# Two squared-ReLU layers: the residual turned to tokens on partitions by VectorE block transposes and transfers

## The chip, the cores and the metric

The kernel runs on one core of one Trainium2 chip. The metric is the device time of one launch in microseconds (us). Before the change it is 1060.97 us, the median of three runs between 1060.56 and 1061.39.

A core has several engines, each with its own stream of instructions: TensorE (PE in the profile, its weight loads PEld), VectorE (DVE), ScalarE (ACT), GpSimd (POOL) and SyncE (SP), which in this kernel issues most of the transfers. SBUF is the memory on the core, with 128 partitions; PSUM holds the results of TensorE.

## The reference

Two layers on 512 tokens of width 1024. Each has a token mixer and then a squared-ReLU MLP, each behind an RMS norm and added to the residual; one norm stands at the end.

```python
for layer in range(DEPTH):                       # DEPTH = 2
    hn = rmsnorm(h, norm_mix[layer])
    if layer % 2 == 0:
        mix = chunked_band_attention(hn, ...)
    else:
        mix = rglru_block(hn, ...)
    h = h + mix
    h = h + sq_relu_mlp(rmsnorm(h, norm_mlp[layer]), mlp_w1[layer], mlp_w2[layer])
return rmsnorm(h, norm_final)

def rmsnorm(x, g):
    return x * rsqrt(mean(x * x, axis=-1) + 1e-6) * g

def sq_relu_mlp(h, w1, w2):                      # w1 1024 x 4096, w2 4096 x 1024
    z = relu(h @ w1)
    return (z * z) @ w2
```

Everything is float32.

## The kernel before

**Layout.** The residual h is kept with features on partitions: eight tiles `hT[k]` of 128 features x 512 tokens, four in each of the buffers `hx0` and `hx1` (in the profile `h`). For a product the value is split in two parts of a shorter float type, `hnH` by ScalarE (L237) and `hnL` by VectorE (L238), and so are all weights: a tile loaded by SP (`wr` or `b`, L120 and L128) is cast to `wh` on ScalarE (L140) and the rest `wl` is formed on VectorE (L143). A product then is three matmuls, high by high, high by low and low by high (`mm3`, L217 to L219). Weights are fetched five tiles ahead from one list, `plan`, in the order of use; the raw tiles of w2 lie in buffers b11, b21, b12 and b22 of the pool `sr`.

**The MLP of a layer** is `mlp(ly, norm)` (L603). `up(p, j)` (L636) is one product of 24 matmuls: 128 of the hidden columns for all 512 tokens, into a bank of PSUM called `u`; ScalarE takes ReLU and square (L643, L644). The norm's factor isn't applied to h: since relu(s h)^2 = s^2 relu(h)^2 for s > 0, the factor `rq` (s squared, one number per token) is applied when results are read. Eight `up`s make one round of four, `round_(p)`. A round multiplies by w2 in seven block products of a Strassen scheme, called "11", "12", "s1", "s4", "s2", "s3" and "22", of 24 matmuls each, on PSUM banks X, Y and Z with tokens on partitions. After each product `read` (L625) adds bank times `rq` into the tiles `d` (128 tokens x 512 features, `dt[t, c]`): four token blocks t, two halves c. In the three first rounds the `up`s of the next round stand between the steps.

**Residual and norm in layer 0 (before).** The first read of each `d` is a ScalarE copy with scale (L629), later reads are VectorE instructions (L631). The sum of squares of the norm is taken from `hT`: eight squares on ScalarE (L244, L247), seven adds on VectorE into `nm1acc` (L248), and small matmuls against a tile of ones (`tokens`, L261, `nm1ss`) which stand after `up(0, 3)`. At the end `turns` (L755) turns `d` back to features on partitions by 32 TensorE transposes (L767, banks `back0` and `back1`), and VectorE adds them to `hT` (L769). The next norm, `n1`, is made of the new `hT` in the same way: eight squares, seven adds, matmuls `n1ss` within the recurrent layer's first products `xb` (L261), and after them `rstd`.

**Residual and norm in layer 1 (before).** The output is wanted with tokens on partitions, so here the residual is turned at the layer's start: after each `up(0, j)`, `turn(t, c)` (L617) makes four TensorE transposes into a bank `hx` (L620), a ScalarE copy into `d` (L621) and a ScalarE square with a sum along the row into a column of `fs` (L623). After `up(0, 7)`, `rq` is formed of the columns. All reads are VectorE's.

**What sets the order.** The program is written in the order above. The Tile framework's scheduler places each instruction in its engine's stream and sets the semaphores; each engine runs its stream in order. A transfer that waits holds back all that stand behind it on SP.

Of the kernel before, what the change touches and what calls it, by code (L numbers as in the profile page):

```python
# [10 lines left out]
F32 = mybir.dt.float32  # L11
F32R = mybir.dt.float32r
AF = mybir.ActivationFunctionType
ALU = mybir.AluOpType
# [26 lines left out]
def trunk(ctx: ExitStack, tc: tile.TileContext, xT, cols, gfin, win, wqkv, wo, rwin, rga, rgx, rwo, w1, w2, out):  # L41
# [13 lines left out]
    def atp(name):  # L55
        return ps.tile([P, T], F32, name=name, tag="at")
# [44 lines left out]
    def fetch():  # L101
# [129 lines left out]
    class Norm:  # L231
# [41 lines left out]
        def inverse(self, total):  # L273
            V.tensor_scalar(rq, total, 1.0 / D, EPS, ALU.mult, ALU.add)
            V.reciprocal(rq, rq)

        def rstd(self):
            row = atp(f"{self.name}row")
            for t in range(4):
                PE.matmul(row[:, t * P : (t + 1) * P], rt[:, t : t + 1].to_broadcast([P, P]), ident, start=True, stop=True)  # L280
            r = self.both[:, 1]
            S.copy(r, row)
            return r
# [319 lines left out]
    def mlp(ly, norm):  # L603
        with ExitStack() as mctx:
# [11 lines left out]

            def turn(t, c):  # L617
                x = atp(f"hx{t}{c}")
                for m in range(4):
                    PE.transpose(x[:, m * P : (m + 1) * P], hT[4 * c + m][:, t * P : (t + 1) * P], ident)  # L620
                S.copy(dt[t, c], x)  # L621
                sq = wk.tile([P, T], F32, name=f"hsq{t}{c}", tag="nsq", bufs=2)
                S.activation(sq, x, AF.Square, accum_out=fs[:, 2 * t + c : 2 * t + c + 1])  # L623

            def read(acc, t, c):  # L625
                d, r = dt[t, c], rq[:, t : t + 1]
                if (t, c) in new:
                    new.remove((t, c))
                    S.activation(d, acc, AF.Copy, scale=r)  # L629
                else:  # L630
                    V.scalar_tensor_tensor(d, acc, r, d, ALU.mult, ALU.add)  # L631

# [3 lines left out]
            def up(p, j):  # L636
                if j % 4 == 0:
                    a[p, j // 4] = zp.tile([P, 2, 4, U], F32, name=f"a{ly}{p}{j}", tag=f"a{j // 4}")
                WH, WL = want(1)
                acc = mmp(f"u{ly}{p}{j}")  # L640
                project([acc], [slice(0, P)], WH, WL, xs)
                c = a[p, j // 4][:, :, j % 4, :]
                S.activation(c, acc.rearrange("p (h c) -> p h c", h=2), AF.Relu)  # L643
# [12 lines left out]
            def round_(p):  # L656
# [95 lines left out]
                step("22", X, False, 2, 0)  # L752


            def turns(step, product, X):  # L755
# [3 lines left out]
                def back(qs, h):  # L759
                    for q in qs:  # L760
# [25 lines left out]
                next(opening)  # L786
                for m in range(4, KT):
                    n1.square(m)
                for _ in open_x(1):
                    pass  # L790
                for m in range(4):
                    n1.square(m)


            def ends(step, product, X):
                gain = [gfins[:, c] for c in range(2)]
                total = lambda t: fs[:, 2 * t : 2 * t + 1]
                part = lambda t, c: fs[:, 2 * t + c : 2 * t + c + 1]

                def squares(t, c):  # L800
                    sq = wk.tile([P, T], F32, name=f"fsq{t}{c}", tag="nsq", bufs=2)
                    S.activation(sq, dt[t, c], AF.Square, accum_out=part(t, c))

# [70 lines left out]
    with ExitStack() as rctx:  # L874
# [83 lines left out]
        for u in range(4):  # L958
            WH, WL = want(2 if u > 1 else 1)
            for i in range(2):  # L960
# [5 lines left out]
                if c == 1:  # L966
                    n1.sums()
                if c == 2:
# [93 lines left out]
```

## Time and profile before

| | |
|---|---|
| median of three runs | 1060.97 us (1060.56 to 1061.39) |
| profiled execution | 1061.19 us |
| its span, first to last instruction | 1059.4 us |
| mean granted TensorE clock | 0.999 |
| TensorE matmuls | 1051.4 us busy, 4824 |
| VectorE | 795.4 us busy, 1174 |
| ScalarE | 587.1 us busy, 899 |
| transfers | 111.51 MB, 105 GB/s on the mean |

The times below are microseconds from the start of the span of that one execution. A row such as `L217 PE MATMUL u<-hnH,wh` names the line of the kernel, the engine, the operation and the tiles that it writes and reads. A row of the timeline begins with its start and its duration. Matmuls run into each other: the duration of one is longer than the distance of two starts.

The MLP of layer 0 runs on TensorE from 245.37, that of layer 1 from 721.93.

### The profile page before, as it was taken

To read this page: it belongs to the slowest core of one execution; us is meant where nothing else is said; L and a number is where in the kernel's file an instruction comes from. 1 tells how busy PE (TensorE), PEld (TensorE's weight loads), DVE (VectorE), ACT (ScalarE), POOL (GpSimd) and SP (SyncE) were. 2 spreads that over 40 slices of the span, in tenths; PEclk is the share of its full clock that TensorE was granted. 3 is DMA by queue.
4 is the path that set the end of the run, shared out by engine and by line. 5 is a ranking of instruction groups with operands and counts; after the bars stand their busy time and mean duration, and the time that the engine had idled before them with its cause. 6 is when DMAs were issued, how large, how long until landed. Compare 5 with 4: busy or idle time off the path is not lost.

```text
span 1059.4 us, 12872 instructions
## 1 busy us (share of the span) xinstructions
PE 1051.4 (99%) x4824; PEld 871.6 (82%) x4824; DVE 795.4 (75%) x1174; ACT 587.1 (55%) x899; POOL 10.1 (1%) x28
## 2 busy tenths in 40 slices
PE   9999999999999999999999999999999999999997
PEld 8888888888888888888888878888888888888886
DVE  6898779867395697587599799974397487577596
ACT  6677557646463564454456587545564454454454
POOL 1010000000000000000000000000000000000000
PEclk9999999999999999999999999999999999999999
DMA  8444353254046036026103222283136026125002
GB/s 263 118 129 130 80 176 103 76 163 160 21 127 188 5 98 200 21 80 199 40 1 115 85 80 86 67 288 97 40 92 200 27 80 198 41 79 179 1 1 80
DMA packets 128413, 111.51 MB, mean 105 GB/s; under 512 B 4320, under 2 KB 104672, under 8 KB 128352
## 3 DMA queue, kind: packets, MB, share of 16 engines
q1 hardware_dynamic: 127776, 109.99, 34.0%
q8 instruction: 38, 0.62, 0.2%
q10 hardware_dynamic: 576, 0.72, 0.2%
q14 instruction: 23, 0.19, 0.1%
HBM read 104.39 MB, written 2.10 MB: 101 GB/s over the span
## 4 chain that ended last, share of the span: by engine, by line
PE 97%; DVE 1%; ACT 1%; issue 0%; DMA 0%; POOL 0%; ACTq 0%; POOLq 0%
PE u L217 11%; PE u L219 11%; PE u L218 11%; PE x L217 6%; PE x L219 5%; PE x L218 5%; PE y L217 3%; PE y L218 3%; PE y L219 3%; PE x L439 2%; PE wo L217 1%; PE wo L218 1%; PE ro L219 1%; PE v L217 1%; PE ro L217 1%; PE xb L217 1%
## 5 line engine op out<-in xcount | busy, mean ns | idle before, releaser
L143 DVE TENSOR_TENSOR wl<-wr,wh 128x1024 fp32r<-128x1024 f32 (+1 forms) x122 | 146.5, 1202 | 98.0 <-ACT wh L140 89.6
L140 ACT CAST wh<-b 128x1024 fp32r<-128x1024 f32 x112 | 117.8, 1052 | 174.2 <-PE u L218 128.1
L140 ACT CAST wh<-wr 128x1024 fp32r<-128x1024 f32 (+1 forms) x121 | 125.6, 1040 | 145.4 <-PE u L218 63.4
L143 DVE TENSOR_TENSOR wl<-b,wh 128x1024 fp32r<-128x1024 f32 x112 | 136.6, 1220 | 91.1 <-ACT wh L140 91.0
L217 PE MATMUL u<-hnH,wh 128*128 128x512 f32 x512 | 200.1, 391 | 0.0
L219 PE MATMUL u<-hnH,wl 128*128 128x512 f32 x512 | 199.4, 389 | 0.0
L218 PE MATMUL u<-hnL,wh 128*128 128x512 f32 x512 | 199.2, 389 | 0.0
L219 PEld LDWEIGHTS u<-hnH,wl 128*128 128x128 f32 x512 | 96.1, 188 | 20.2
L218 PEld LDWEIGHTS u<-hnL,wh 128*128 128x128 f32 x512 | 96.2, 188 | 19.8
L217 PEld LDWEIGHTS u<-hnH,wh 128*128 128x128 f32 x512 | 96.1, 188 | 19.7
L138 DVE TENSOR_TENSOR b<-b,b 128x1024 f32<-128x1024 f32 x64 | 76.3, 1216 | 1.1 <-DMA b<-in_w 0.8
L217 PE MATMUL x<-wh,h 128*128 128x512 f32 (+1 forms) x132 | 50.8, 385 | 0.6 <-DVE d L836 0.6
L218 PE MATMUL x<-wl,h 128*128 128x512 f32 (+1 forms) x132 | 50.6, 384 | 0.0
L643 ACT ACTIVATE a<-u 128x512 f32<-128x512 f32 x64 | 37.8, 591 | 13.3 <-PE u L219 13.3
L631 DVE SCALAR_TENSOR_TENSOR d<-x,rq,d 128x512 f32<-128x512 f32 x59 | 42.0, 744 | 0.5 <-PE x L219 0.5
L644 ACT ACTIVATE a<-a 128x512 f32<-128x512 f32 x64 | 40.6, 635 | 1.7
L419 ACT ACTIVATE p<-p,mx 128x128 f32<-128x128 f32 (+1 forms) x64 | 35.2, 552 | 6.2 <-DVE mx L416 6.1
L667 ACT CAST h<-a 128x1024 fp32r<-128x1024 f32 (+2 forms) x34 | 27.2, 800 | 6.7 <-PE y L218 5.8
L412 DVE CUSTOM_DVE_ANT_0 p<-s,bias 128x128 f32<-128x128 f32 (+1 forms) x64 | 27.6, 484 | 3.2 <-PE s L409 2.9
L217 PEld LDWEIGHTS x<-wh,h 128*128 128x128 f32 x132 | 24.8, 188 | 5.5 <-DVE d L836 0.8
L443 ACT CAST pH<-x 128x512 fp32r<-128x512 f32 (+1 forms) x48 | 21.7, 517 | 13.5 <-PE x L439 13.3
L218 PEld LDWEIGHTS x<-wl,h 128*128 128x128 f32 x132 | 24.8, 188 | 4.8
(351 smaller groups left out, 2292.4 us busy)
## 6 DMA issues: line engine op xcount, KB each, us to landing
wr<-in_w SPq DMA_DIRECT2D x64, 512.0 KB, 4.1
b<-in_w SPq DMA_DIRECT2D x64, 512.0 KB, 4.3
wr<-in_wqkv SPq DMA_DIRECT2D x20, 512.0 KB, 4.0
wr<-in_rwin SPq DMA_DIRECT2D x16, 512.0 KB, 3.4
wr<-in_wo SPq DMA_DIRECT2D x8, 512.0 KB, 4.1
wr<-in_rwo SPq DMA_DIRECT2D x8, 512.0 KB, 3.5
x<-in_xT SPq DMA_DIRECT2D x8, 256.0 KB, 3.8
bias<-in_win SPq DMA_DIRECT2D x4, 512.0 KB, 4.7
```

The costliest lines, as they stand in the source:

```text
L138: V.tensor_sub(raw, raws[x, half], raws[y, half])
L140: S.copy(H[:, :n], raw[:, :n])
L143: low = V.tensor_sub(L[:, :n], raw[:, :n], f(H[:, :n]))
L217: PE.matmul(acc, WH, XH, start=start, stop=False, skip_group_check=more)
L218: PE.matmul(acc, WH, XL, start=False, stop=False, skip_group_check=more)
L219: PE.matmul(acc, WL, XH, start=False, stop=stop, skip_group_check=more)
L412: V.tensor_tensor_reduce(out=pt[:, seg[t] : seg[t] + n], in0=sc[t], in1=b[:, h % 4, T - n :], scale=1.0, scalar=-3.0e38, op0=ALU.add, op1= ...
L419: S.activation(pt[:, seg[t] : seg[t] + n], pt[:, seg[t] : seg[t] + n], AF.Exp, bias=mx[:, t : t + 1], accum_out=sm[:, t : t + 1],)
L631: V.scalar_tensor_tensor(d, acc, r, d, ALU.mult, ALU.add)
L643: S.activation(c, acc.rearrange("p (h c) -> p h c", h=2), AF.Relu)
L644: S.activation(c, c, AF.Square)
L667: S.copy(H[:, ks], raw[n][:, ks])
```

## The change

In both MLP layers the residual now is in `d` from the start.

- **Turning.** `turn()` stands after `up(0, 0)`. VectorE transposes `hT` in blocks of 32 x 32: 16 instructions of 128 partitions x 8 x 32 elements, into two tiles `turned`, which take the place of the raw weights b12 and b22 before these are loaded. A block transpose moves elements within 32 partitions only; 32 transfers on SP, SBUF to SBUF, 32 partitions x 2 x 256 elements each (64 KB), bring the blocks to the partitions of their tokens, into `res`, of which the tiles `dt[t, c]` are views. Within a token's row the features come out in another order; the host puts the rows and columns of the weights, the gains and the output in the order that fits (`once` for layer 1's input, `twice` for the end).
- **Norm sums.** Eight ScalarE squares of `d` with sums along the row into columns of `fs`, written in the program after `up(0, 5)`, and `rq` of them after `up(0, 6)`: in both layers. The norm `n1` takes its sums in the same way from the finished `d` at the end of layer 0, with one VectorE add of columns. So `nm1ss`, `n1ss`, `hx`, and the adds `nm1acc` and `n1acc` are gone.
- **Reads.** All reads are VectorE's, eight more in layer 0 and as many fewer on ScalarE.
- **Turning back.** The 32 TensorE transposes at the end of layer 0 stay. VectorE copies the result to `hT` instead of adding it.
- **Raw weights.** b11, b21, b12 and b22 are tiles of two halves each, instead of two tiles each.

```diff
+                    both = state["raw"].tile([P, 2, 1024], F32, name=f"b{name}_{i}", tag=f"b{name}")
                     for h in range(2):
-                        raws[name, h] = state["raw"].tile([P, 1024], F32, name=f"b{name}{h}_{i}", tag=f"b{name}{h}")
+                        raws[name, h] = both[:, h]
...
-        def sums(self):
-            S.activation(rt, self.tokens(), AF.Sqrt, bias=epsb, scale=1.0 / D)
+        def sums(self, total=None):
+            S.activation(rt, self.tokens() if total is None else total, AF.Sqrt, bias=epsb, scale=1.0 / D)
             V.reciprocal(rt, rt)
...
-            dt = {(t, c): dp.tile([P, T], F32, name=f"d{ly}{t}{c}", tag=f"d{t}{c}") for t in range(4) for c in range(2)}
-            new = set() if ly else set(dt)
+            res = dp.tile([P, 4, 2, T], F32, name=f"d{ly}", tag="d")
+            dt = {(t, c): res[:, t, c] for t in range(4) for c in range(2)}
...
-            def turn(t, c):
-                x = atp(f"hx{t}{c}")
-                for m in range(4):
-                    PE.transpose(x[:, m * P : (m + 1) * P], hT[4 * c + m][:, t * P : (t + 1) * P], ident)
-                S.copy(dt[t, c], x)
-                sq = wk.tile([P, T], F32, name=f"hsq{t}{c}", tag="nsq", bufs=2)
-                S.activation(sq, x, AF.Square, accum_out=fs[:, 2 * t + c : 2 * t + c + 1])
+            def turn():
+                blocks = [sr.tile([P, 2, 4, KT, 32], F32, name=f"turned{ly}{h}", tag=f"b{n}2") for h, n in enumerate((1, 2))]
+                for k in range(KT):
+                    for h in range(2):
+                        V.transpose(
+                            blocks[h].rearrange("p t j k a -> p (t j) k a")[:, :, k],
+                            hT[k][:, h * U : (h + 1) * U].rearrange("p (n b) -> p n b", b=32),
+                        )
+                for h in range(2):
+                    for i in range(4):
+                        for j in range(4):
+                            nc.sync.dma_start(
+                                res[32 * j : 32 * j + 32, 2 * h : 2 * h + 2, i // 2, (i % 2) * U : (i % 2 + 1) * U],
+                                blocks[h][32 * i : 32 * i + 32, :, j].rearrange("p t k a -> p t (k a)"),
+                            )
 
             def read(acc, t, c):
                 d, r = dt[t, c], rq[:, t : t + 1]
-                if (t, c) in new:
-                    new.remove((t, c))
-                    S.activation(d, acc, AF.Copy, scale=r)
-                else:
-                    V.scalar_tensor_tensor(d, acc, r, d, ALU.mult, ALU.add)
+                V.scalar_tensor_tensor(d, acc, r, d, ALU.mult, ALU.add)
...
-                if p == 0 and ly:
-                    turn(*divmod(j, 2))
-                if (ly, p, j) == (0, 0, 0):
-                    for k in range(KT):
-                        norm.square(k)
-                elif (ly, p, j) == (0, 0, 3):
-                    norm.inverse(norm.tokens())
-                elif (ly, p, j) == (1, 0, 7):
+                if (p, j) == (0, 0):
+                    turn()
+                if (p, j) == (0, 5):
+                    for t in range(4):
+                        for c in range(2):
+                            squares(t, c)
+                if (p, j) == (0, 6):
                     V.tensor_add(rq, fs[:, 0:8:2], fs[:, 1:8:2])
-                    norm.inverse(rq)
+                    V.tensor_scalar(rq, rq, 1.0 / D, EPS, ALU.mult, ALU.add)
+                    V.reciprocal(rq, rq)
...
+            def squares(t, c):
+                sq = wk.tile([P, T], F32, name=f"dsq{ly}{t}{c}", tag="nsq", bufs=2)
+                S.activation(sq, dt[t, c], AF.Square, accum_out=part(t, c))
...
-                        V.tensor_add(hv, x.rearrange("p (i c) -> p i c", i=2), hv)
+                        V.tensor_copy(hv, x.rearrange("p (i c) -> p i c", i=2))
...
-                for m in range(4, KT):
-                    n1.square(m)
+                for t in range(4):
+                    squares(t, 1)
+                for t in range(2):
+                    squares(t, 0)
                 for _ in open_x(1):
                     pass
-                for m in range(4):
-                    n1.square(m)
+                for t in range(2, 4):
+                    squares(t, 0)
...
                 if c == 1:
-                    n1.sums()
+                    V.tensor_add(rt, fs[:, 0:8:2], fs[:, 1:8:2])
+                    n1.sums(rt)
```

How the instructions now stand, at three places. The first is TensorE at the start of layer 1's MLP, the end of `up(0, 0)` and the start of `up(0, 1)` (banks `u100` and `u101`). Before:

```order
L217 MATMUL u100_6237<-hnH7_83,wh146_6069 128x512
L218 MATMUL u100_6237<-hnL7_91,wh146_6069 128x512
L219 MATMUL u100_6237<-hnH7_83,wl146_6070 128x512
L620 MATMUL hx00_6264<-ident_92,h0_1564 128x128 x4
L217 MATMUL u101_6278<-hnH0_76,wh147_6075 128x512
L218 MATMUL u101_6278<-hnL0_84,wh147_6075 128x512
```

Now:

```order
L218 MATMUL u100_6236<-hnH7_83,wh146_6075 128x512
L219 MATMUL u100_6236<-hnL7_91,wh146_6075 128x512
L220 MATMUL u100_6236<-hnH7_83,wl146_6076 128x512
L218 MATMUL u101_6319<-hnH0_76,wh147_6081 128x512
L219 MATMUL u101_6319<-hnL0_84,wh147_6081 128x512
```

The four transposes between the two products are gone, and so are those behind the seven other `up`s. (Lines behind L128 count one more or a few fewer in the new kernel.)

The second place is VectorE around the end of the attention part in layer 0, where the last products `wo` are added to h and the last operands `hnL` for the first `up` are formed. Before:

```order
L238 SCALAR_TENSOR_TENSOR hnL4_88<-h1_1565,cst_73,hnH4_80 128x512
L362 TENSOR_TENSOR h1_1565<-wo45_2509,h1_1565 128x512
L143 TENSOR_TENSOR wl37_2526<-wr37_2527,wh37_2525 128x1024
L238 SCALAR_TENSOR_TENSOR hnL5_89<-h1_1565,cst_73,hnH5_81 128x512
L362 TENSOR_TENSOR h1_1565<-wo46_2531,h1_1565 128x512
L248 TENSOR_TENSOR nm1acc_2626<-nm1acc_2626,nm1sq2_2631 128x512
L362 TENSOR_TENSOR h1_1565<-wo47_2547,h1_1565 128x512
L238 SCALAR_TENSOR_TENSOR hnL6_90<-h1_1565,cst_73,hnH6_82 128x512
L143 TENSOR_TENSOR wl38_2588<-wr38_2589,wh38_2587 128x1024
L238 SCALAR_TENSOR_TENSOR hnL7_91<-h1_1565,cst_73,hnH7_83 128x512
```

Now, from `hnL5` on:

```order
L239 SCALAR_TENSOR_TENSOR hnL5_89<-h1_1565,cst_73,hnH5_81 128x512
L358 TENSOR_TENSOR h1_1565<-wo46_2531,h1_1565 128x512
L618 STREAM_TRANSPOSE turned00_2619<-h0_1564 128x8x32
L618 STREAM_TRANSPOSE turned01_2620<-h0_1564 128x8x32
L618 STREAM_TRANSPOSE turned00_2619<-h0_1564 128x8x32
L239 SCALAR_TENSOR_TENSOR hnL6_90<-h1_1565,cst_73,hnH6_82 128x512
L358 TENSOR_TENSOR h1_1565<-wo47_2547,h1_1565 128x512
L618 STREAM_TRANSPOSE turned01_2620<-h0_1564 128x8x32
L144 TENSOR_TENSOR wl38_2581<-wr38_2582,wh38_2580 128x1024
L618 STREAM_TRANSPOSE turned00_2619<-h0_1564 128x8x32
L239 SCALAR_TENSOR_TENSOR hnL7_91<-h1_1565,cst_73,hnH7_83 128x512
```

Five transposes stand between the add of `wo46` and the last `hnL`, two more stand ahead of the add of `wo45`, and nine come behind `hnL7`. The adds `nm1acc` are gone.

The third place is SP in layer 1. The loads `wr148` to `wr153` are the weights of `up(0, 2)` to `up(0, 7)`, b12 and b22 raw weights of w2. Before:

```order
L120 DMA wr148_6137<-in_w1 128x8x128
L128 DMA b220_154_6368<-in_w2 128x2x512
L128 DMA b221_154_6370<-in_w2 128x2x512
L120 DMA wr149_6143<-in_w1 128x8x128
L120 DMA wr150_6227<-in_w1 128x8x128
L120 DMA wr151_6233<-in_w1 128x8x128
L120 DMA wr152_6274<-in_w1 128x8x128
L120 DMA wr153_6315<-in_w1 128x8x128
L120 DMA wr160_6603<-in_w1 128x8x128
```

Now:

```order
L120 DMA wr151_6232<-in_w1 128x8x128
L120 DMA wr152_6315<-in_w1 128x8x128
L625 DMA d1_6222<-turned10_6263 32x2x256 x16
L625 DMA d1_6222<-turned11_6264 32x2x256 x16
L120 DMA wr153_6348<-in_w1 128x8x128
L129 DMA b12_154_6387<-in_w2 128x2x512 x2
L129 DMA b22_154_6390<-in_w2 128x2x512 x2
L120 DMA wr160_6600<-in_w1 128x8x128
```

The 32 transfers stand ahead of the load for `up(0, 7)` and of those of b12 and b22. In layer 0 they stand behind the load for `up(0, 7)` and ahead of b12 and b22.

More of the change, by code (lines that the diff above doesn't have):

```diff
@@ L280, in rstd @@
                 PE.matmul(row[:, t * P : (t + 1) * P], rt[:, t : t + 1].to_broadcast([P, P]), ident, start=True, stop=True)
-            r = self.both[:, 1]
+            r = wk.tile([P, 2, T], F32, name=f"{self.name}r", tag="nn")[:, 1] if self.acc is None else self.both[:, 1]
             S.copy(r, row)
@@ L752, in round_ @@
                 step("22", X, False, 2, 0)
+            total = lambda t: fs[:, 2 * t : 2 * t + 1]
+            part = lambda t, c: fs[:, 2 * t + c : 2 * t + c + 1]
+            def squares(t, c):
+                sq = wk.tile([P, T], F32, name=f"dsq{ly}{t}{c}", tag="nsq", bufs=2)
+                S.activation(sq, dt[t, c], AF.Square, accum_out=part(t, c))
             def turns(step, product, X):
@@ L1034, in col @@
         return v.reshape(-1, P).T
+    once = np.arange(D).reshape(KT, 4, 32).transpose(1, 0, 2).reshape(-1)
+    twice = once[once]
     cols = np.concatenate(
-        [col(a["norm_mix"][0]), col(a["norm_mlp"][0]), col(a["norm_mix"][1]), col(a["norm_mlp"][1]),
+        [col(a["norm_mix"][0]), col(a["norm_mlp"][0]), col(a["norm_mix"][1][once]), col(a["norm_mlp"][1][once]),
          col(a["rec_b_in"][0]), col(a["rec_conv_w"][0]), col(a["rec_conv_b"][0]),
-         col(a["rec_b_ga"][0]), col(a["rec_b_gx"][0]), col(a["rec_a_param"][0]), col(a["rec_b_o"][0])],
+         col(a["rec_b_ga"][0]), col(a["rec_b_gx"][0]), col(a["rec_a_param"][0]), col(a["rec_b_o"][0][once])],
         axis=1,
@@ L1046 @@
     arrs = {
[L1047 to L1049 removed]
+        "xT": a["x"][0].T, "cols": cols, "gfin": np.broadcast_to(a["norm_final"][twice], (P, D)), "win": win, "wqkv": a["attn_w_qkv"][0], "wo": a["attn_w_o"][0],
+        "rwin": a["rec_w_in"][0][once], "rga": a["rec_w_ga"][0], "rgx": a["rec_w_gx"][0], "rwo": a["rec_w_o"][0][:, once],
+        "w1": np.stack([a["mlp_w1"][0], a["mlp_w1"][1][once]]),
+        "w2": np.stack([a["mlp_w2"][0][:, once], a["mlp_w2"][1][:, twice]]),
     }
@@ L1060 @@
     r = _run(nc, [arrays], core_ids=[0])
-    return r.results[0]["out_0"][None]
+    return r.results[0]["out_0"][None][:, :, np.argsort(twice)]
```

11 lines of the change are left out of this document (removed).

## The prediction

> **What bounds the kernel now.** I read the page first: the span, the busy shares and the chain that ended last; then TensorE's own waits. The three rows after the chain are every wait of TensorE that the view of waits names (who waited, for what, and the us in total, the times, the longest).
>
> ```profile
> span 1059.4 us, 12872 instructions
> PE 1051.4 (99%) x4824; PEld 871.6 (82%) x4824; DVE 795.4 (75%) x1174; ACT 587.1 (55%) x899; POOL 10.1 (1%) x28
> PE 97%; DVE 1%; ACT 1%; issue 0%; DMA 0%; POOL 0%; ACTq 0%; POOLq 0%
> ...
> PE warm L472 <- POOL ones L85: 1.0, 1, 1.0
> PE x L217 <- DVE d L836: 0.6, 1, 0.6
> PE s L408 <- DMA kl<-kl: 0.3, 1, 0.3
> ```
>
> TensorE is busy for 99% of the span, 97% of the last chain is its own work, and it waits 1.9 us in all. So an edit pays only by what it takes out of TensorE's row of matmuls, and costs only where it makes that row wait. What VectorE, ScalarE and the queues gain or lose counts for nothing until something reaches TensorE late.
>
> **The unit.** A stretch of layer 1 without anything special, the first matmul of a product and the same place seven products of 24 matmuls later (timeline: start, duration):
>
> ```profile
> 829.29 0.39 PE L217 MATMUL u<-hnH,wh 128*128 128x512 f32 x1
> ...
> 867.37 0.39 PE L217 MATMUL u<-hnH,wh 128*128 128x512 f32 x1
> ```
>
> 38.08 / 7 = 5.44 us a product, 0.2267 a matmul. Each MLP layer opens with eleven such products (eight `up`, then steps "11", "12", "s1"), which should last 59.84 us. The start of the first `up` and of what follows the eleventh, in layer 0 and in layer 1:
>
> ```profile
> 245.37 0.39 PE L217 MATMUL u<-hnH,wh 128*128 128x512 f32 x1
> ...
> 306.18 0.39 PE L217 MATMUL u<-hnH,wh 128*128 128x512 f32 x1
> ...
> 721.93 0.40 PE L217 MATMUL u<-hnH,wh 128*128 128x512 f32 x1
> ...
> 785.77 0.39 PE L217 MATMUL u<-hnH,wh 128*128 128x512 f32 x1
> ```
>
> Layer 0 takes 60.81, 0.97 more than its products; the only other TensorE work in there is the norm's column sum `nm1ss`. Layer 1 takes 63.84, 4.00 more; there it is the 32 transposes of `hx`.
>
> ```profile
> L620 PE MATMUL hx<-ident,h x32: 270/272/273, 727.4 to 769.3; 128*128 128x128 f32 x32
> ```
>
> The row says 272 ns each, but they overlap: on TensorE's path one costs 4.00 / 32 = 0.125 us. The Trainium skill, page "VectorE: DVE Perf Modes", section "Rules for kernel authors", says to transpose 128x128 on TensorE when the result may go to PSUM; its section "The three transpose paths" gives 390 ns there and 311 ns for VectorE's 32x32 blocks (bf16). By that rule the change would gain nothing; the trace differs, since in this kernel TensorE is the one engine with no room.
>
> The third removal is the recurrent layer's column sum:
>
> ```profile
> 592.94 0.39 PE L219 MATMUL xb<-hnH,wl 128*128 128x512 f32 x1
> 593.17 0.95 PE L261 MATMUL n1ss<-ones,n1acc 128*128 128x2 f32 x8
> 593.98 0.49 PE L217 MATMUL xb<-hnH,wh 128*128 128x512 f32 x1
> 594.30 0.40 PE L218 MATMUL xb<-hnL,wh 128*128 128x512 f32 x1
> ```
>
> From 592.94 to 594.30 are 1.36 us where two matmuls need 0.45: 0.91. **Gain: 4.00 + 0.97 + 0.91 = 5.88 us.**
>
> **What it adds: VectorE at the starts of the layers.** 16 transposes of 128 partitions x 256 elements per layer. The trace has no such instruction. The nearest rows of that shape, and other VectorE and ScalarE prices used below (busy us, mean ns):
>
> ```profile
> L426 DVE TENSOR_SCALAR p<-p,sm 128x256 f32<-128x256 f32 x16 | 5.6, 347 | 0.0
> L444 DVE TENSOR_TENSOR pL<-x,pH 128x256 fp32r<-128x256 f32 x16 | 6.6, 412 | 0.0
> ...
> L631 DVE SCALAR_TENSOR_TENSOR d<-y,rq,d 128x512 f32<-128x512 f32 x28 | 19.9, 740 | 0.0
> ...
> L140 ACT CAST wh<-wr 128x1024 fp32r<-128x1024 f32 x118 | 123.8, 1051 | 144.7 <-PE u L218 63.4 <-PE x L219 19.6 <-PE ro L218 12.2
> L143 DVE TENSOR_TENSOR wl<-wr,wh 128x1024 fp32r<-128x1024 f32 x118 | 143.8, 1220 | 98.0 <-ACT wh L140 89.6 <-DMA wr<-in_w 8.0
> ...
> L623 ACT ACTIVATE hsq<-hx 128x512 f32<-128x512 f32 x8 | 4.8, 597 | 0.0
> L643 ACT ACTIVATE a<-u 128x512 f32<-128x512 f32 x64 | 37.8, 591 | 13.3 <-PE u L219 13.3
> ```
>
> I take T = 0.41 us, the two-operand row, because a transpose can hardly beat one operand in and one out (0.35) by much; the upper bound is half its rate, 0.82. Over both layers VectorE gains 32 x 0.41 = 13.1 us and eight reads of 0.74, and loses 14 adds of 0.68: +9.5 us on 795. That total is harmless; the place isn't. Layer 0's eighth operand pair decides when the first `up` can run on:
>
> ```profile
> 239.51 1.22 DVE L138 TENSOR_TENSOR b<-b,b 128x1024 f32<-128x1024 f32 x1
> ...
> 243.71 0.68 DVE L362 TENSOR_TENSOR h<-wo,h 128x512 f32<-128x512 f32 x1
> 244.31 0.68 DVE L248 TENSOR_TENSOR nm1acc<-nm1acc,nm1sq 128x512 f32<-128x512 f32 x1
> 245.57 0.69 DVE L362 TENSOR_TENSOR h<-wo,h 128x512 f32<-128x512 f32 x1 [0.58 <-PE wo L219]
> 246.18 0.74 DVE L238 SCALAR_TENSOR_TENSOR hnL<-h,cst,hnH 128x512 fp32r<-128x512 f32 x1
> 246.84 1.22 DVE L143 TENSOR_TENSOR wl<-wr,wh 128x1024 fp32r<-128x1024 f32 x1
> 247.97 0.74 DVE L238 SCALAR_TENSOR_TENSOR hnL<-h,cst,hnH 128x512 fp32r<-128x512 f32 x1
> ...
> 250.37 0.39 PE L218 MATMUL u<-hnL,wh 128*128 128x512 f32 x1
> ```
>
> The last row is the first matmul that needs the last `hnL`, ready before at 248.71. After the change two transposes stand ahead of the add at 243.71, and the subtraction of `b` (1.14 to the next start) and an add like that at 244.31 (0.60) are gone from before it: 241.97 + 2T. Behind it come the add 0.60, three transposes, `hnL6` 0.66, the last add 0.61, T, `wl` 1.13, T, `hnL7` 0.74: ready at 245.71 + 7T. For T = 0.41 that is 248.6 (248.9 with the last add's wait for `wo` until 245.57); TensorE waits only if 7T > 4.66, that is T > 0.66. The skill's 311 ns per 128 columns would make an estimate of T = 0.62 here, still in time; no run yet shows it.
>
> Layer 1, the same place:
>
> ```profile
> 722.13 0.75 DVE L1006 SCALAR_TENSOR_TENSOR h<-ro,cst,h 128x512 f32<-128x512 f32 x1 [0.62 <-PE ro L219]
> ...
> 726.97 0.39 PE L218 MATMUL u<-hnL,wh 128*128 128x512 f32 x1
> ```
>
> After the last `ro` add stand T, one `wl`, T and `hnL7`: 722.13 + 0.75 + T + 1.22 + T + 0.74 = 724.84 + 2T, in time up to T = 1.06. Cost of the transposes: 0.
>
> **What it adds: 32 transfers per layer on SP.** 64 KB each, inside SBUF. The nearest are the moves of `kh` and `kl` from one half of the partitions to the other (x2 is two transfers in one row; the page's rows give KB each and us to landing):
>
> ```profile
> 77.10 1.11 SPq L323 DMA_DIRECT2D kh<-kh  x2
> 78.43 1.18 SPq L324 DMA_DIRECT2D kl<-kl  x2
> 79.66 0.59 SPq L120 DMA_DIRECT2D wr<-in_wqkv  x1
> ...
> kh<-kh SPq DMA_DIRECT2D x16, 128.0 KB, 2.2
> wr<-in_w SPq DMA_DIRECT2D x64, 512.0 KB, 4.1
> ```
>
> Four in 2.56 us is 0.64 each, landing 2.2 after the issue though the next is already out. 32 of them hold SP for 20.5 us. Queued behind them on SP: in layer 1 the weight load of `up(0,7)`, then the loads of b12 and b22; in layer 0 those two. Waiting for them on ScalarE: the eight squares of the landed tiles, which stand between the casts and ReLUs of the `up`s.
>
> Layer 1: the last block is transposed at 723.3 (722.88 + T), `up(0,7)` starts at 721.93 + 7 x 5.44 = 760.0, and its weights need landing 4.1, cast 1.05, subtraction 1.22, so the load must be issued by 753.6. The transfers may take t = 30.3 / 32 = 0.95 each; at 0.64 there are 9.8 us left.
>
> Layer 0: the last block is ready at about 252.3 (hnL7 at 248.9, nine T, less pipelining), the last square can start 32t + 2.2 later. On ScalarE three squares of 0.6, three weight casts and six pieces of about 0.6 (ReLUs, their squares and the split of a) stand from there to the second half of step "12"'s operand, and one subtraction of 0.68 on VectorE: 9.2 in all. That half is wanted at 306.18 - 2 x 5.44 + 2.72 = 298.0. So 252.3 + 32t + 2.2 + 9.2 < 298.0, up to t = 1.07; at 0.64 there are 13.8 us left. The product of b12 minus b11, wanted at 300.74, gives 1.21 in the same way (load 4.1, cast, two subtractions). `rq`, from the squares, is wanted by the read of step "11" at about 295 and 771, over ten us after them. Cost 0.
>
> **What it adds elsewhere: reads and the end of layer 0.** Layer 0's first round has eight more reads on VectorE, 5.9 us. The stretch (columns: us, then busy time of PE, PEld, DVE, ACT, POOL, clock, DMA share, GB/s):
>
> ```profile
> 289.30:343.00 53.70, 53.70 (x239) 44.48 (x238) 40.41 (x39) 30.08 (x36) 0.00 (x0) 1.00 0.49 148
> ```
>
> 46.3 of 53.7 still fits, with the reads spread over six products. At the end of layer 0 the transposes back to feature-major stay; between their second and third group stand three matmuls instead of seven, 0.91 us less cover for emptying a bank. A copy (0.68, as the add) behind a read (0.74) may leave TensorE waiting 0.74 at worst, in three places 2.2; I take 0.1 as the reads are due earlier.
>
> **Sum.** The profiled execution took 1061.19 us, 0.22 above the median of 1060.97. 1061.19 - 5.88 = 1055.31; from the median 1055.09. I take **1055.2**.
>
> **The rivals.** (a) Forecast: nothing arrives late; 1055.2. (b) VectorE's transposes run at half rate or less, T = 0.82 to 1.0: layer 0's `hnL7` comes at 251.45 to 252.71, so TensorE waits 1.1 to 2.3: 1056.3 to 1057.5. For it: 32-bit data through a block transpose is in no row. Against: T has to pass 0.66. (c) VectorE in layer 0's first round, or the end of layer 0, gives part back: between 2.2 (the end alone) and 5.9 (every added read reaches TensorE): 1057.4 to 1061.1. Against: 13 us idle in that window. (d) The other side: the transfers don't overlap. Each has 64 runs of 1 KB and touches a quarter of the partitions, where a move of `kh` has 64 runs of 2 KB and touches half. Once they take t > 0.95 each, `up(0,7)` waits 32 x (t - 0.95), and past 1.07 layer 0 as well; at t = 1.12 the gain is gone, at 1.3 it is 11.2 + 7.4 = 18.6: 1073.8. With 2.2 each, strictly in turn, 40 + 36 = 76: 1131. For it: small runs, and the weights' loads share the engines (DMA share 0.49). Against: `kh`'s pitch of 0.64 at twice the bytes. The Trainium skill, page "DMA: Bandwidth & Descriptors", section "Rules for kernel authors", says that transfers to disjoint partition parts serialize and that under 64 KB one pays mostly overhead; by it (d) would be near. The trace of `kh`, whose four overlap, speaks against strict turns.
>
> **Chances.** A measurement of this kernel can tell about 0.2%, 2.1 us, from no change: faster is below 1058.85. (a) 0.70, (b) 0.09, both faster; (c) 0.11, of which 0.04 faster and 0.07 same, as its upper part lies past 1058.85; (d) 0.10, slower, nearly all past 1063.1. Faster 0.83, same 0.07, slower 0.10. Range: down to 1054.0 (the runs' half spread 0.4 and 0.8 for column sums that cost more than their own place shows); up to 1058.5, which holds (a), (b) and the lower third of (c) with the spread.
>
> **What would show it.** Right: no `hx`, `nm1ss` or `n1ss` on TensorE; the eleven first products in 59.8 us in both layers; no new wait of TensorE above 0.3; a transpose near 0.41; `d<-turned` issued 0.6 to 0.7 apart. Wrong: `hnL7` after its matmul's due time (b); TensorE waiting for DVE `d` or `ls` before 343, or in the `back` groups (c); transfers over 0.95 apart and TensorE waiting for `wl` of `up(0,7)` near 760 (d).

## The result, and the profile after

The changed kernel takes 1055.11 us (median of six runs, 1054.63 to 1055.39); the kernel before, in six runs beside it, 1060.95 (1060.07 to 1061.39). The ratio is 0.9942, with a 95% interval of 0.9932 to 0.9952: 5.8 us faster.

The page of the changed kernel, its span, busy shares and chain, and then all waits of TensorE (who waited, for what, us in total, times, longest):

```profile
span 1052.7 us, 12906 instructions
PE 1044.9 (99%) x4776; PEld 866.4 (82%) x4776; DVE 802.8 (76%) x1202; ACT 581.6 (55%) x899; POOL 9.8 (1%) x28
PE 98%; DVE 1%; ACT 1%; DMA 0%; issue 0%; POOL 0%; ACTq 0%; POOLq 0%
...
PE warm L468 <- POOL ones L85: 1.0, 1, 1.0
PE x L218 <- DVE d L841: 0.6, 1, 0.6
PE s L404 <- DMA kl<-kl: 0.3, 1, 0.3
```

The three waits are those of before, to the tenth. TensorE has 6.5 us less to do, VectorE 7.4 more, and TensorE waits for nothing that it did not wait for already. The eleven first products of each MLP layer lie between these pairs of rows (timeline: start, duration):

```profile
244.72 0.39 PE L218 MATMUL u<-hnH,wh 128*128 128x512 f32 x1
...
304.58 0.39 PE L218 MATMUL u<-hnH,wh 128*128 128x512 f32 x1
...
719.24 0.39 PE L218 MATMUL u<-hnH,wh 128*128 128x512 f32 x1
...
779.09 0.39 PE L218 MATMUL u<-hnH,wh 128*128 128x512 f32 x1
```

59.86 and 59.85 us: eleven times 5.44, with nothing else in between. Now VectorE where the first `up` of layer 0 wants its last operand, and that operand's first use on TensorE:

```profile
L618 DVE STREAM_TRANSPOSE turned<-h 128x256 f32<-128x256 f32 x32 | 11.9, 420 | 0.1
...
246.99 0.44 DVE L618 STREAM_TRANSPOSE turned<-h 128x256 f32<-128x256 f32 x1
247.35 0.75 DVE L239 SCALAR_TENSOR_TENSOR hnL<-h,cst,hnH 128x512 fp32r<-128x512 f32 x1
248.02 3.05 DVE L618 STREAM_TRANSPOSE turned<-h 128x256 f32<-128x256 f32 x9
...
249.73 0.39 PE L219 MATMUL u<-hnL,wh 128*128 128x512 f32 x1
```

A transpose takes 0.42 us; `hnL7` is ready at 248.10, 1.63 before it is wanted. And SP, with the 32 transfers of each layer in one row, the load of the eighth product's weights behind them in layer 1, and the page's row on landing:

```profile
250.81 21.54 SPq L625 DMA_DIRECT2D d<-turned  x32
...
720.74 21.70 SPq L625 DMA_DIRECT2D d<-turned  x32
742.54 0.53 SPq L120 DMA_DIRECT2D wr<-in_w  x1
...
d<-turned SPq DMA_DIRECT2D x64, 64.0 KB, 2.0
```

0.67 to 0.68 us per transfer, landing 2.0 us after the issue, so three are under way at a time. That load goes out at 742.54; the eighth product starts at 719.24 + 38.1 = 757.3.

### The profile page after: what moved, and what is told of

Same layout as the page of the kernel before. It is cut to its first block, busy times and chain, and to the rows that moved or that the text cites. A ratio compares the mean times of both kernels' runs of the same rounds, so it can differ in the third digit from the quotient of the medians.

```text
span 1052.7 us, 12906 instructions
## 1 busy us (share of the span) xinstructions
PE 1044.9 (99%) x4776; PEld 866.4 (82%) x4776; DVE 802.8 (76%) x1202; ACT 581.6 (55%) x899; POOL 9.8 (1%) x28
## 4 chain that ended last, share of the span: by engine, by line
PE 98%; DVE 1%; ACT 1%; DMA 0%; issue 0%; POOL 0%; ACTq 0%; POOLq 0%
PE u L218 11%; PE u L219 11%; PE u L220 11%; PE x L218 6%; PE x L219 6%; PE x L220 6%; PE y L218 3%; PE y L219 3%; PE y L220 3%; PE x L435 2%; PE wo L218 1%; PE wo L219 1%; PE ro L219 1%; PE v L218 1%; PE ro L218 1%; PE wo L220 1%
## 5 line engine op out<-in xcount | busy, mean ns | idle before, releaser
L644 ACT ACTIVATE a<-u 128x512 f32<-128x512 f32 x64 | 37.8, 591 | 30.9 <-PE u L220 30.9
L632 DVE SCALAR_TENSOR_TENSOR d<-x,rq,d 128x512 f32<-128x512 f32 x63 | 44.9, 745 | 2.3 <-PE x L220 2.3
```

## The experiments

The theory: only TensorE's row counts, so the gain is what the edit takes out of it, and the rest is free as long as SP's row and VectorE's stay inside their margins. The rivals: part of the gain is relief on other engines; the transfers, or VectorE's transposes, are nearer to costing something than their rows say.

A table that serves for all runs: the lengths of five stretches of TensorE's row, from the starts of matmuls as in the rows above. A is the first `up` of layer 0 to the first matmul behind its step "s1"; B from there to the first product `xb` of the recurrent layer; C from there to the first `up` of layer 1; D is A's twin in layer 1; E goes on to the end of the last matmul.

| kernel | start of A | A | B | C | D | E |
|---|---|---|---|---|---|---|
| before | 245.37 | 60.81 | 269.73 | 146.02 | 63.84 | 267.87 |
| after | 244.72 | 59.86 | 269.53 | 145.13 | 59.85 | 267.89 |
| turn by TensorE in layer 1 | 245.28 | 59.89 | 269.55 | 145.09 | 63.82 | 267.89 |
| sums by TensorE | 244.45 | 60.84 | 269.60 | 146.03 | 59.89 | 267.91 |
| 48 transfers | 244.30 | 60.60 | 269.54 | 145.14 | 61.41 | 267.87 |
| 64 transfers | 245.36 | 67.45 | 269.60 | 145.11 | 73.06 | 267.91 |
| 64, half on GpSimd's queue | 245.45 | 59.89 | 269.64 | 145.10 | 59.89 | 267.87 |
| longer transposes | 244.50 | 59.89 | 269.53 | 145.05 | 59.89 | 267.88 |
| issue on ScalarE | 244.88 | 65.86 | 269.53 | 145.12 | 63.94 | 267.91 |
| quarter of turn back by transfers | 245.02 | 59.89 | 268.66 | 146.04 | 59.85 | 267.88 |
| the same, own buffers | 244.96 | 59.89 | 268.53 | 145.46 | 59.89 | 267.87 |
| the same, and earlier | 244.93 | 59.89 | 268.91 | 145.27 | 59.85 | 267.91 |

Stretches that an edit doesn't touch agree within about 0.1 us from one kernel to the next, one execution of each. The start of A, behind the attention part that no kernel here changes on TensorE, scatters by 1.15 us, and the times contain it. The runs were also made on several chips, each beside its own runs of the kernel before (medians 1060.88 to 1061.19). So below a microsecond the stretches decide, not the medians.

**The turn by TensorE again, in layer 1 alone**

```diff
+                if p == 0 and ly:
+                    turn_pe(*divmod(j, 2))          # the old turn(t, c): 4 transposes, copy, square
-                if (p, j) == (0, 0):
+                if (ly, p, j) == (0, 0, 0):
                     turn()
...
-    twice = once[once]
+    twice = once
```

> Layer 1 turns its residual by 32 TensorE transposes again; layer 0 stays as changed. Theory (only TensorE's row counts): the 32 transposes come back at 0.125 us each, 4.0 us, so 1055.1 + 4.0 = 1059.1, and layer 1's eleven first products last 63.8 us instead of 59.85. Rival (a good part of the gain comes from what the change does on other engines and queues: raw weights in two tiles, the load of the final gains earlier, ScalarE's copies gone): these stay in this kernel, so less than half of the 4.0 comes back, at most 1057.

Measured: 1059.56 us, ratio to the kernel before 0.9985 (0.9977 to 0.9994). D is 63.82: the 32 transposes cost 3.97. The median lies 4.45 above that of the changed kernel, in which the start of A takes part (245.28 against 244.72). The eight `up`s with their transposes begin 5.93 us apart, where 5.44 is usual: eight times the same 0.50. The rival falls, though not by what the expectation says: of the three things that it names, only the tiles of two halves stayed as changed. Layer 1's eight copies are back on ScalarE, and the gains are loaded at 761.51 (763.66 before, 708.55 in the changed kernel). What rules these two out is TensorE's own list: it has no wait for ScalarE or for that load, in this kernel or in the one before, so the 3.97 us are the transposes' own time.

**The norm sums by TensorE again**

```diff
+                if (ly, p, j) == (0, 0, 0):
+                    for k in range(KT):
+                        norm.square(k)
+                if (ly, p, j) == (0, 0, 3):
+                    V.tensor_scalar(rq, norm.tokens(), 1.0 / D, EPS, ALU.mult, ALU.add)
+                    V.reciprocal(rq, rq)
...
-                    n1.sums(rt)
+                    n1.sums()
```

> Both norm sums are taken by TensorE again from squares of h (eight ScalarE squares and seven VectorE adds each, matmuls against ones); the turning stays as changed. Theory: 0.97 + 0.91 come back, 1055.1 + 1.9 = 1057.0, and layer 0's eleven first products last 60.8 again; the seven adds cost nothing. Rival (small matmuls fit in gaps, or the sums' cost was something else): 1055.1 to 1055.5. Second rival (the adds now stand beside the transposes on VectorE and come late): above 1058.

Measured: 1056.36 us, ratio 0.9958 (0.9945 to 0.9970). A is 60.84 (+0.98) and C 146.03 (+0.90), together 1.88 as expected; the median shows 1.25 of it, with A starting 0.27 earlier. Both rivals fall.

**More transfers: 48 and 64 of them, the bytes unchanged**

```diff
+                            for n in (slice(0, 1), slice(1, 2)):
-                            nc.sync.dma_start(
-                                res[32 * j : 32 * j + 32, 2 * h : 2 * h + 2, ...],
-                                blocks[h][32 * i : 32 * i + 32, :, j]...,
+                                nc.sync.dma_start(
+                                    res[32 * j : 32 * j + 32, 2 * h + n.start : 2 * h + n.stop, ...],
+                                    blocks[h][32 * i : 32 * i + 32, n, j]...,
```

(for 48 with the second half of the tokens alone)

> Half of the transfers are split in two halves of 32 KB, so 48 per layer instead of 32, the bytes unchanged. Theory (SP is held by the count, 0.67 us each): SP is held for 32.5 us; in layer 1 the load for the eighth first product is issued at 753.3 and its weights are ready at 759.7 against 757.3, 2.3 late; layer 0 is ready at 294.3 against 296.4. So 1055.1 + 2.3 = 1057.4. Rival (bytes decide, or transfers are hidden anyway): 1055.1, with 64 KB in the same time as before. Rival (in turn, 2 us each): over 1090.

> All transfers are split in two halves of 32 KB, 64 per layer, the bytes unchanged. Theory (by the count, 0.67 us each): SP is held for 43.3 us; layer 1 waits 770.5 - 757.3 = 13.2 us for the weights of the eighth first product, layer 0 waits 305.1 - 296.4 = 8.7 us for the operand of step 12 behind the last squares, together 1055.1 + 21.9 = 1077. Rival (bytes decide): 1055.1. Rival (only the load behind the transfers matters, not the squares): 1068.

Measured with 48: 1057.45 us, ratio 0.9967 (0.9953 to 0.9980). SP in layer 1, the wait of ScalarE's square behind the transfers, the two waits of TensorE that are new, and the window behind the one in layer 1 (its third last number is the granted clock):

```profile
721.08 31.33 SPq L626 DMA_DIRECT2D d<-turned  x48
752.50 0.53 SPq L120 DMA_DIRECT2D wr<-in_w  x1
...
753.13 0.63 ACT L762 ACTIVATE dsq<-d 128x512 f32<-128x512 f32 x1 [4.87 <-DMA d<-turned]
...
PE u L220 <- DVE wl L144: 0.5, 1, 0.5
PE y L220 <- DVE ls L670: 0.4, 1, 0.4
...
759.00:761.00 2.00, 1.87 (x8) 1.58 (x9) 2.00 (x4) 2.00 (x4) 0.00 (x0) 1.00 1.05 391
```

The load comes 10 us later than with 32, and TensorE now waits for `wl` of the eighth product. But it also waits in layer 0, for `ls`, the low part of step "s1"'s operand: A is 0.74 longer where the expectation had none, D 1.56 longer where it had 2.3. The sum was met by luck, its parts were not.

The list gives 0.9 us of waits, and the two stretches are 2.3 longer, at a granted clock of 1.00. TensorE's starts around the wait for `wl` show why:

```profile
757.45 0.39 PE L220 MATMUL u<-hnH,wl 128*128 128x512 f32 x1
757.87 0.50 PE L218 MATMUL u<-hnH,wh 128*128 128x512 f32 x1
758.20 0.40 PE L219 MATMUL u<-hnL,wh 128*128 128x512 f32 x1
759.13 0.50 PE L220 MATMUL u<-hnH,wl 128*128 128x512 f32 x1 [0.53 <-DVE wl L144]
759.46 0.39 PE L218 MATMUL u<-hnH,wh 128*128 128x512 f32 x1
```

The list counts from the end of the matmul ahead (758.20 + 0.40), but in a row the next one would have started 0.23 behind its start: 0.70 are lost, not 0.53. The starts around it come late too: the four distances are 2.01 us in all where 0.91 is usual, 1.1 us lost. The rest of D's 1.56 is mostly at `ls` of step "s1" in layer 1 (starts at 775.35, 775.85 and 776.18), by a gap too short for the list.

Measured with 64: 1076.32 us, ratio 1.0145 (1.0131 to 1.0159). SP in layer 1, the two long waits of TensorE, one window behind the wait in layer 0 and those around the one in layer 1 (columns: us, busy time of PE, PEld, DVE, ACT, POOL, then the granted clock, DMA share, GB/s):

```profile
729.02 41.32 SPq L626 DMA_DIRECT2D d<-turned  x64
770.45 0.52 SPq L120 DMA_DIRECT2D wr<-in_w  x1
...
PE u L218 <- ACT wh L141: 10.1, 1, 10.1
PE z L218 <- ACT h L669: 4.1, 1, 4.1
...
302.00:308.00 6.00, 5.74 (x15) 4.14 (x14) 6.00 (x8) 5.20 (x7) 0.00 (x0) 0.55 0.73 212
...
760.00:768.00 8.00, 5.78 (x26) 4.46 (x24) 2.50 (x4) 3.58 (x7) 0.00 (x0) 1.00 0.19 53
768.00:776.00 8.00, 0.09 (x1) 0.09 (x1) 0.62 (x4) 3.13 (x8) 0.00 (x0) 0.52 0.58 185
776.00:780.00 4.00, 4.00 (x10) 3.17 (x11) 4.00 (x4) 2.88 (x4) 0.00 (x0) 0.50 1.06 392
780.00:784.00 4.00, 4.00 (x15) 3.27 (x14) 4.00 (x4) 2.10 (x2) 0.00 (x0) 0.76 1.09 327
784.00:788.00 4.00, 4.00 (x19) 3.30 (x18) 1.30 (x3) 2.83 (x5) 0.00 (x0) 1.00 0.03 8
```

Half the bytes in a transfer change its hold on SP only from 0.67 to 0.65 us, so it is the count that holds SP: bytes don't decide, and turns of 2 us don't happen. D is 13.21 longer, the number of the expectation, but by luck, as it is made differently: the wait is 10.1 (the product starts on `wh`, without the `wl` that I had added, and the transfers take 0.65), and 3.1 us more go, nearly all because TensorE comes out of it with a granted clock of 0.50 and gets back to 1.00 only by 784. In layer 0 the wait of 4.1 for the operand of step "12", the place that was expected, costs A 7.59 in the same way, with one of 0.3 right behind it.

The Trainium skill, page "TensorE: Matmul & The Clock Gate", section "Part 1: The HAM clock gate", describes such a clock: throttled by default and released by activity. The windows agree: 0.50 behind the wait of 10.1 us and 0.55 behind that of 4.1. Behind the wait of 0.5 in the run with 48 the window shows 1.00.

**64 transfers, half of them issued by GpSimd**

```diff
-                                nc.sync.dma_start(
+                                (nc.gpsimd if n.start else nc.sync).dma_start(
```

> The same 64 transfers of 32 KB per layer as in the run with 64, but every second one is issued by GpSimd, which does nothing else there. Theory (what costs is the time that SP's row is held, by the count): SP is held for 32 x 0.65 = 21 us as in the changed kernel, and as long as GpSimd needs less than 0.95 us for each of its own, nothing is late: 1055.1. Rival (the transfer engines or the small pieces are the limit, whoever issues): about 1076 again. No row shows yet what a transfer from GpSimd's queue costs; over 1.1 us each would leave a part of the loss.

Measured: 1054.88 us, ratio 0.9942 (0.9927 to 0.9957). Both rows in layer 0:

```profile
251.53 21.01 SPq L626 DMA_DIRECT2D d<-turned  x32
...
252.26 15.77 POOL L626 DMA_DIRECT2D d<-turned  x32 [82.93 <-ACT wh L141]
```

The same 64 pieces, and the 21 us are gone. What cost time was the row of SP, not the transfers. GpSimd needs 0.49 us for each.

**Longer transposes**

```diff
-                            blocks[h].rearrange("p t j k a -> p (t j) k a")[:, :, k],
-                            hT[k][:, h * U : (h + 1) * U].rearrange("p (n b) -> p n b", b=32),
+                            blocks[h].rearrange("p t j k a -> p (t j) k a")[:, :, k : k + w],      # w = min(3, KT - k)
+                            hT[k][:, h * U : (h + 1) * U].rearrange("p (n u b) -> p n u b", u=1, b=32).to_broadcast([P, 8, w, 32]),
```

> VectorE's transposes read each block up to three times (768 columns instead of 256 for six of eight tiles, 512 for one); the surplus is overwritten by the next ones. A long one should take about 0.95 us, so VectorE gets some 7 us more per layer, and as the instructions are ordered four of them stand ahead of layer 0's last operand pair, which is then ready at 248.9 against 249.7, and the last transfers land some 6 us later, inside the 13 us of margin. Theory (the transposes are off the path): 1055.1. Rival (VectorE's time at the starts of the layers is on the path): 1058 to 1069.

Measured: 1054.65 us, ratio 0.9942 (0.9929 to 0.9956). The tile's row gives the least, the middle and the longest duration in ns; below it layer 0's last operand:

```profile
L619 DVE STREAM_TRANSPOSE turned<-h x32: 407/943/974, 238.1 to 725.1; 128x768 f32<-128x768 f32 x24, 128x512 f32<-128x512 f32 x4, 128x256 f32<-128x256 f32 x4
...
247.31 0.74 DVE L239 SCALAR_TENSOR_TENSOR hnL<-h,cst,hnH 128x512 fp32r<-128x512 f32 x1
```

Transposes of 0.94 us cost nothing. Of the longer ones three stand ahead of `hnL7`, not the four that the expectation names and not the seven of the changed kernel: the scheduler gave another order; `hnL7` is ready at 248.05, as with the short ones. So case (b) of the prediction, which kept seven ahead, would not have come with longer transposes alone.

**The transfers issued by ScalarE**

```diff
-                            nc.sync.dma_start(
+                            nc.scalar.dma_start(
```

> The 32 transfers of a layer are issued by ScalarE instead of SP, in one block between the first ReLUs. Theory (an issue holds its engine's row for about 0.65 us): ScalarE is held for 21 us from 250.8 on; the cast of the weights for the fifth first product follows at 272.3, these are ready at 274.6 against 266.5, so layer 0 waits 8 us; in layer 1 the cast behind the block is for the seventh product, in time. 1055.1 + 8 = 1063. Rival (an issue is over at once and only SP's own order counted): 1055.1 or a little less, since the loads behind no longer wait.

Measured: 1064.82 us (seven runs between 1061.73 and 1065.56), ratio 1.0030 (1.0020 to 1.0041), slower than the kernel before. ScalarE in layer 0, its queue's row and the next instruction, what TensorE waited for, and three windows behind its wait in layer 1:

```profile
251.88 22.82 ACTq L625 DMA_DIRECT2D d<-turned  x31
274.74 1.04 ACT L141 CAST wh<-wr 128x1024 fp32r<-128x1024 f32 x1 [22.23 <-DMA d<-turned]
...
PE u L218 <- ACT a L644: 6.3, 2, 4.1
...
755.00:756.00 1.00, 1.00 (x2) 0.81 (x3) 0.79 (x2) 1.00 (x2) 0.00 (x0) 0.50 0.00 0
756.00:758.00 2.00, 2.00 (x6) 1.61 (x5) 1.28 (x2) 2.00 (x4) 0.00 (x0) 0.50 0.96 287
...
759.00:762.00 3.00, 3.00 (x15) 2.47 (x14) 1.97 (x3) 3.00 (x5) 0.00 (x0) 1.00 1.07 328
```

ScalarE does nothing for 22 us. The theory holds in kind; its places were wrong. TensorE waits in both layers (A +6.00, D +4.09) and not for the cast of weights but for banks that the held ReLU (L644) had not emptied: 6.3 us of waits, nearly all the rest of the 10.1 at a lower clock. The wait in layer 1 was only 2.2 us long (6.3 less 4.1), and it too was followed by a granted clock of 0.50.

**A version that goes on: a quarter of the turn back by transfers**

The experiments say that TensorE's row is the time and that GpSimd's queue is free. At the end of layer 0, 32 transposes remain on TensorE. Eight of them (tokens 0 to 255, features 0 to 511) have their data long before.

```diff
...
                 step("12", Z, True, 0, 0)
+                if p == 3 and not ly:
+                    part_ = [wk.tile([P, T], F32, name=f"part{t}", tag="nsq", bufs=2) for t in range(2)]
+                    for t in range(2):
+                        V.transpose(part_[t].rearrange("p (n b) -> p n b", b=32), dt[t, 0].rearrange("p (n b) -> p n b", b=32))
+                    for t in range(2):
+                        for g in range(4):
+                            for r in range(4):
+                                nc.gpsimd.dma_start(
+                                    hx_[0][32 * r : 32 * r + 32, :, t * P + 32 * g : t * P + 32 * g + 32],
+                                    part_[t][32 * g : 32 * g + 32].rearrange("p (m r b) -> p m r b", r=4, b=32)[:, :, r],
+                                )
...
-                back(range(4), 0)
+                back((2, 3), 0)
```

> At the end of layer 0, eight of the 32 TensorE transposes back to features on partitions (features 0 to 511, tokens 0 to 255, complete since step 12 of the last round) are replaced by two VectorE block transposes of 128 x 512 and 32 transfers of 16 KB from GpSimd's queue, straight into h. Theory (TensorE's row): 8 x 0.125 = 1.0 us less, 1054.1, if the transfers take less than 0.88 us each from about 547 on, since these tiles of h are wanted at 577.7. Rival (runs of 128 bytes or the queue are slow): with 1.5 us each TensorE waits 20 us less what later products cover, over 1060. Rival (the transposes back stand beside waits anyway): 1055.1.

Measured: 1055.48 us, ratio 0.9951 (0.9938 to 0.9963): nothing gained, B + C is 414.70 against 414.66. Eight transposes less, and a new wait. The tile `part` took the two buffers of ScalarE's squares:

```profile
570.34 0.63 ACT L773 ACTIVATE dsq<-d 128x512 f32<-128x512 f32 x1 [1.65 <-DMA h<-part]
...
PE xb L220 <- DVE hnL L240: 0.3, 1, 0.3
```

A square had to wait until the transfers had read its buffer, and behind the squares ScalarE splits h. Two more runs told this from the other suspect, the place of the transposes:

```diff
-                    part_ = [wk.tile([P, T], F32, name=f"part{t}", tag="nsq", bufs=2) for t in range(2)]
+                    part_ = [sr.tile([P, T], F32, name=f"part{t}", tag=f"part{t}") for t in range(2)]
```

> As the run before with a quarter of the turn back by transfers, but the two transposed tiles lie in buffers of their own, so that no square on ScalarE has to wait for the transfers that read them (that wait was 1.65 us, ahead of the split of h). Theory A (that wait delayed the operands hnL of the first recurrent product, which TensorE then waited for): the wait goes and 1.0 is gained: 1054.1. Theory B (the operands are late because the second group of transposes back stands too late on TensorE, and the chain copy, hnH, hnL behind it has less work to hide under): the operands come at the same time, 1055.1 to 1055.5.

and with `back((2, 3), 1)` moved ahead of the first half of step "22":

> Own buffers, and the second group of transposes back stands ahead of the first half of step 22 in the program; on TensorE it comes about 1 us earlier, eight matmuls behind the first group instead of twelve. Theory A and theory B: hnL is in time and the 8 x 0.125 stay gained, 1054.1; the stretch from layer 0's second round to layer 1 is 413.7 instead of 414.7. If the chain is bound elsewhere (VectorE's read of the last banks): 1055.1.

Measured: own buffers 1054.76 us, ratio 0.9942 (0.9929 to 0.9956), B + C 413.99; and earlier 1054.46, ratio 0.9937 (0.9924 to 0.9949), B + C 414.18. The wait for `hnL` is gone from TensorE's list in both, so theory A holds for the wait, and the earlier place adds nothing. Of the 1.0 us that the theory promised, 0.67 and 0.48 are gained in the traces, and where the rest goes is not shown; the times, inside each other's scatter with the changed kernel's 1055.11, can't show it. Both versions beat the kernel before.

## Why the prediction was right, point by point

- **The gain.** Transposes 4.00 predicted, 3.99 in D; `nm1ss` 0.97, 0.95 in A; `n1ss` 0.91, 0.89 in C. Undone one by one, they came back as 3.97, 0.98 and 0.90. With B's 0.20, where a loss of 0.1 had been taken, the stretches give 6.0 and the medians 5.84 against 5.88. The 0.20 lies at the `back` groups at the end of layer 0: their new order, which was to cost, gained a little.
- **VectorE at the starts.** T was taken as 0.41 and is 0.42, not the 0.62 of the other estimate, and in a row the starts are closer still: nine in 3.05 us. VectorE's total is 7.4 us up where 9.5 were summed. `hnL7` was put 3.5 us behind the first `up`'s start (248.9 - 245.37) and comes 3.4 behind it (248.10 - 244.72).
- **SP.** 0.64 predicted, 0.67 measured; landing 2.2 and 2.0. The load behind has 8.4 us left (757.3 - 6.4 - 742.54) where 9.8 were predicted.
- **Reads on VectorE.** The window of layer 0's first round, 1.4 us earlier as the round is, is now

```profile
287.90:341.60 53.70, 53.70 (x239) 44.46 (x238) 44.04 (x45) 26.86 (x30) 0.00 (x0) 1.00 0.48 149
```

  44.0 us of VectorE where 46.3 were allowed for, and TensorE without a gap. Case (c) did not happen.
- **What was off.** The prices of rival (d), which did not come to pass in the change, but did in the runs with more transfers. Its point for layer 0, 1.07 us per transfer, came from the operand of step "12". With 31.31 us on SP, the same as 0.98 for each of 32, layer 0 already waits, for `ls` of step "s1", a chain that I had not worked out. And its loss counted waits alone: a wait of 10.1 us costs 13.2, since the granted clock is 0.50 behind it. By its own prices the gain would have been gone at t = 1.10, not 1.12: 32 x (1.10 - 0.95) + 32 x (1.10 - 1.07) = 5.8.
- **Transfers in turn.** 32 transfers to quarters of the partitions go out every 0.67 us with 2.0 to landing. So the rule of the Trainium skill, page "DMA: Bandwidth & Descriptors", section "Rules for kernel authors", that two transfers to disjoint partition halves serialize, does not hold here as rival (d) read it, as turns of the whole landing time. Whether the pieces move one behind the other within the 2.0 us, no run shows.
- **Transposes.** VectorE's instruction for two blocks of 128 columns takes 0.42 us and needs the transfers besides, against 0.25 of TensorE's path for two transposes, but it lies beside the row that is the time.

What stays open is the start of A. The attention part, with the same matmuls, takes between 244.3 and 245.45 us from one execution to the next. The traces show where most of that arises: in the first microseconds of the kernel, before anything that the change touches. In the twelve traces the 101st matmul already starts between 22.40 and 23.67 us. The first four matmuls `qk`, in the kernel before and in the run with 48 transfers:

```profile
5.32 1.91 PE L500 MATMUL qk<-hnH,wh 128*128 128x512 f32 x4
...
5.16 1.17 PE L496 MATMUL qk<-hnH,wh 128*128 128x512 f32 x4
```

The next group of four starts 1.75 us behind them in the first (7.07) and 1.01 in the second (6.17), which is 0.44 and 0.25 a matmul. Behind three such groups the two kernels are 0.91 us apart (8.90 and 7.99), of the 1.07 at the start of A. 0.44 is near the 0.43 a matmul that the run with 64 shows at a granted clock of 0.50, so the clock is the suspect. It is not shown: the view gives 1.00 there.

## What to carry to other kernels

When one engine is busy for 99% of the span, work moved off it pays its price on that engine's own row (the distance of starts with and without it, here 0.125 us where the record says 0.27), however costly it is elsewhere, as long as each place it moves to has its deadline worked out. Small transfers are paid for by their number, in the row of the engine that issues them: put them on a queue behind which nothing waits. And the wait that you cause costs more than its length in the list: here 1.1 us where the list says 0.5, and, once it is long enough for the clock to fall (2.2 us were enough), some microseconds more.

## What the runs showed of the hardware

- A transfer inside SBUF holds SP for 0.67 us at 64 KB, 0.65 at 32 KB; GpSimd 0.49 at 32 KB; ScalarE 0.74 at 64 KB, in which it computes nothing.
- VectorE's block transpose of 128 x 256 float32 takes 0.42 us, of 128 x 768 0.94; in a row they start 0.33 us apart in the small form.
- Behind a wait of TensorE of 10.1 us the granted clock was 0.50 for some 6 us, behind one of 4.1 us it was 0.55 over the next 6; behind one of 2.2 us it was 0.50 for some 3; behind one of 0.5 us it stayed at 1.00.
- Without any fall of the clock, the wait of 0.5 us delayed TensorE by 1.1: the list counts from the end of a matmul's record, and the starts around a wait are 0.33 us apart in place of 0.23.
